# A two-layer encoder trunk on one core: engine order by deadline, buffers from common pools

## The chip, the core and the metric

The kernel runs on one core of a Trainium2 chip. The core has TensorE (PE in the profile, with PEld for its weight loads), VectorE (DVE), ScalarE (ACT), GpSimd (POOL) and SyncE (SP, which here issues almost all DMA). Each engine runs its own instructions in program order and waits on semaphores for the others. The metric is the device time of one execution in microseconds (us). The kernel before takes 858.26 us, the median of three runs (857.68 to 860.0).

## What is computed

Two layers are applied to x, 256 tokens of 2048 channels. All is float32. Cut to what matters:

```python
def hybrid_layer(x, c, cos, sin, layer_idx, w_ada, b_ada, ...):
    mod = (c @ w_ada + b_ada)[:, None, :]
    shift, scale, gate = jnp.split(mod, 3, axis=-1)
    h = rms_norm(x, g_pre) * (1 + scale) + shift
    z = h @ w_in                                    # 2048 x 6144
    u, g_pool, q, k, v, g_diff = jnp.split(z, splits, axis=-1)
    pool_out = multiscale_pool(u, w_pool, pool_scale) * jax.nn.silu(g_pool)
    q, k = apply_rope(q, cos, sin), apply_rope(k, cos, sin)
    att = diff_attention(q, k, v, lam)              # 8 heads, two softmaxes each
    att = rms_norm(att, subln_g) * (1.0 - lam_init)
    diff_out = att.reshape(B, S, D_DIFF) * jax.nn.silu(g_diff)
    y = jnp.concatenate([pool_out, diff_out], axis=-1) @ w_out   # 2048 x 2048
    return x + (1 + gate) * rms_norm(y, g_post)
```

`c @ w_ada` gives 6144 numbers per layer for one vector c; its weights, 50 MB per layer, are as many bytes as w_in's.

## The kernel before

The 256 tokens are two row halves of 128 (`st` 0 and 1), x0 and x1. The large products w_in and w_out are cut into 256 **units**: one unit is a 512 KB piece of weights, 256 rows by 512 columns (`Unit`, with its column block `nb` and its pair of row tiles `k`). w_in has 12 column blocks of 8 units per layer, w_out has 4. Both sides of every product are split in two: `whi`, the weights rounded by an ACT cast, and `wlo`, the rest, raw − whi, by DVE. A unit is then 12 products of 128x512 on PE (24 of 128x256 where the result is wanted transposed): hi by hi, hi by lo and lo by hi. h, the normed and modulated x, is split the same way (`hhi`, `hlo`).

`c @ w_ada` is done on DVE: 192 instructions (`ada`), each multiplying a 512 KB piece by the broadcast c and summing along the row. `ab` makes the columns A and B from them, by which h of a row tile is modulated; so h of row-tile pair `kp` waits for its ada rows, and w_in's units are ordered in visits to the column blocks as h becomes ready. Where a block is visited more than once, its sum is copied out of the accumulator (z<-acc) and back into another (acc<-z), on ACT but for a few of the copies back.

Beside the units run: the rotation of q and k (`rope`), four pairs of attention heads per layer (`heads`), four pooling groups (`pool_group`), the gate's columns turned into a broadcast row `G` (`gate`), and h itself (`make_h`). These are generators. `advance` steps them between units, each when a rough clock (`Clock`) says that its last step is over; `beside` lets them and the ada rows in after each unit, the ada rows by a credit per unit (`RATE`), and `split_to` casts a unit's weights `DEEP` = 2 units ahead. A block's heads begin when its Q, K, V and gate blocks are all done. Buffers are fixed pools by purpose: 12 of z, 9 of h and cat, 4 raw, 3 each of whi and wlo, 3 ada.

The reciprocal square root for the norms before w_in in layer 0 and for the heads is made on POOL (`rsqrt`, with a guess on DVE), that for the residuals on DVE (`rms`).

At the end of a layer, `turn_over` places everything by hand. The last four units of w_out run for half 0 first, then half 1 (`group`). While PE does half 1, half 0 is gated (`end_y`), its residual is added to x0 (`residual`) and squared. Then come half 1's gating, half 0's norm and h (`half_h`), and half 1's residual follows in between. The first four units of layer 1 run for half 0, then for half 1. The ada rows go on during the whole of both layers.

All instructions are issued through one helper, so the profile gives L86 for every row; a row is found by its tile names.

Of the kernel before, what the change touches and what calls it, by code (L numbers as in the profile page):

```python
# [19 lines left out]
DEPTH = 2  # L20
S = 256
# [40 lines left out]
class Unit:  # L62
    def __init__(self, w, l, nb, k, first, last, more):
        self.w, self.l, self.nb, self.k = w, l, nb, k
        self.first, self.last, self.more = first, last, more
        self.extras = []
        self.group, self.far, self.quiet = 0, False, False


class Watched:  # L70


    def __init__(self, clock, key, eng):
        self.clock, self.key, self.eng = clock, key, eng

    def __getattr__(self, name):
        f = getattr(self.eng, name)

        def call(*args, **kw):
# [3 lines left out]
            if "out" not in kw:  # L83
                outs.append(aps.pop(0))
            self.clock.note(self.key, outs, aps + list(named.values()))
# [5 lines left out]
class Clock:  # L91


    FIXED = {"tensor": 0.0, "vector": 0.07, "scalar": 0.09, "gpsimd": 0.15, "sync": 0.0}
    EACH = {"tensor": 0.42e-3, "vector": 1.04e-3, "scalar": 0.85e-3, "gpsimd": 2.3e-3, "sync": 1.43e-3}

    def __init__(self, nc):
        self.now = dict.fromkeys(self.FIXED, 0.0)
        self.wrote, self.used, self.last = {}, {}, 0.0
        for k in self.FIXED:  # L100
            setattr(self, k, Watched(self, k, getattr(nc, k)))

    def note(self, key, outs, ins):
        n = math.prod(outs[0].shape[1:])
        if key == "sync":
            n *= outs[0].shape[0] / P
        if key == "tensor" and ins[-1].dtype == F32:
            n *= 4 if len(ins) == 2 and ins[-1].shape[-1] != P else 2
        t = self.now[key]
        for x in ins:  # L110
            t = max(t, self.wrote.get(x.tensor.name, 0.0))
        for x in outs:
            if key != "tensor":
                t = max(t, self.used.get(x.tensor.name, 0.0))
        t += self.FIXED[key] + n * self.EACH[key]
        self.now[key] = t
        done = t + (1.5 if key == "sync" else 0.15)
        for x in ins:
            self.used[x.tensor.name] = max(self.used.get(x.tensor.name, 0.0), t)
        for x in outs:  # L120
            self.wrote[x.tensor.name] = self.used[x.tensor.name] = done
        self.last = max(self.last, done)


class Kern:
    def __init__(self, ctx, tc, a, out):
        self.tc, self.nc, self.a, self.out = tc, Clock(tc.nc), a, out
        pool = lambda name, bufs, **kw: ctx.enter_context(tc.tile_pool(name=name, bufs=bufs, **kw))
        self.cp = pool("cp", 1)
        self.sp = pool("sp", 2)  # L130
# [7 lines left out]
        self.accp = pool("accp", 4, space=PSUM)  # L138
        self.psp = pool("psp", 4, space=PSUM)
        self.dp = pool("dp", 2, space=bass.MemoryType.DRAM)  # L140
        self.names = 0
        self.live = 0

    def name(self, s):
        self.names += 1
        return f"{s}{self.names}"

    def t(self, pool, shape, tag, dt=F32, **kw):
        return pool.tile(shape, dt, tag=tag, name=self.name(tag), **kw)

    def ps(self):
        self.live += 1
        return self.t(self.psp, [P, 512], "ps")
# [1036 lines left out]
```

## Time and profile before

| | |
|---|---|
| median of three runs | 858.26 us (857.68, 858.26, 860.0) |
| the profiled execution | 856.63 us, span 854.8 us |
| bytes read | 242.17 MB |
| first product of a unit | 25.16 us |
| last w_out product of layer 0 ends, first w_in product of layer 1 | 436.4, 443.74 us |
| last w_out product of layer 1 ends | 844.71 us |

The span runs from the first to the last instruction of the profiled execution; the time of a run is a little longer. The page gives busy time per engine; a window gives the same for a stretch of the span, with the granted clock of PE (PEclk) and what the DMA engines moved. A group row gives all instructions of one kind: how many, their sum in us, the mean of one in ns, and the idle time of the engine right before them with what ended it. In a timeline row the first number is the start, the second the length in us, and the bracket the wait before it.

### The profile page before, as it was taken

The numbers are of one execution on the slowest core, as the hardware profiler recorded it, in microseconds if no ns is written. First come the engines' busy times: TensorE is split into PE (matmuls) and PEld (weight loads), VectorE is DVE, ScalarE is ACT, GpSimd is POOL, SyncE is SP. The second block draws the span as 40 slices with busy tenths as digits, with TensorE's granted clock in tenths as the row PEclk, the third lists the DMA queues.
The fourth block names the chain that finished last, engine by engine and source line by source line (L and its number), as shares of the span: only waits on it lengthen the run. The fifth ranks groups of instructions, "written<-read, shape, count | busy, mean of one in ns | idle before, by whom it ended". The sixth has DMA issues, their size and how long they took to land.

```text
span 854.8 us, 11938 instructions
## 1 busy us (share of the span) xinstructions
PE 803.6 (94%) x4058; PEld 667.5 (78%) x4058; DVE 695.5 (81%) x1194; ACT 543.5 (64%) x950; POOL 45.8 (5%) x129
## 2 busy tenths in 40 slices
PE   3899899999999999998979999999999999889995
PEld 1678688889888887786758888888889898677884
DVE  6789898888898977988786788888789989667665
ACT  4688787766556666664655656776665567666561
POOL 2000000000000001142000000000000000030400
PEclk9999999999999999999989999999999999999998
DMA  9899999999898975688925999999998888443742
GB/s 340 287 396 327 330 370 344 370 367 350 304 355 325 331 251 166 207 287 292 324 73 182 343 365 383 326 346 322 357 326 333 309 320 265 130 148 109 261 148 99
DMA packets 68239, 245.08 MB, mean 287 GB/s; under 512 B 7729, under 2 KB 8017, under 8 KB 67665
## 3 DMA queue, kind: packets, MB, share of 16 engines
q1 hardware_dynamic: 67890, 244.14, 80.3%
q8 instruction: 32, 0.52, 0.3%
q10 hardware_dynamic: 288, 0.17, 0.1%
q14 instruction: 29, 0.24, 0.1%
HBM read 242.17 MB, written 2.11 MB: 286 GB/s over the span
## 4 chain that ended last, share of the span: by engine, by line
PE 75%; DVE 10%; ACT 5%; DMA 4%; POOL 3%; issue 2%; SPq 0%; DVEq 0%; ACTq 0%
PE acc L86 69%; PE ps L86 6%; DVE wlo L86 3%; ACT whi L86 2%; POOL arh L86 2%; DVE ada L86 2%; DMA raw<-in_w_out 1%; ACT t L86 1%; DMA z<-in_w_ada 1%; DVE z L86 1%; DMA ada<-in_w_ada 1%; DVE rt L86 1%; DMA raw<-in_w_in 1%; DVE x L86 1%; ACT sqj L86 1%
## 5 line engine op out<-in xcount | busy, mean ns | idle before, releaser
L86 ACT CAST whi<-raw 128x1024 fp32r<-128x1024 f32 x247 | 259.4, 1053 | 205.1 <-PE acc L86 182.7
L86 DVE TENSOR_TENSOR wlo<-raw,whi 128x1024 fp32r<-128x1024 f32 x247 | 301.3, 1223 | 81.2 <-ACT whi L86 80.7
L86 PE MATMUL acc<-whi,hhi 128*128 128x512 f32 x860 | 344.3, 400 | 6.0 <-ACT hhi L86 2.5
L86 PE MATMUL acc<-whi,hlo 128*128 128x512 f32 x860 | 337.8, 393 | 1.3 <-DVE hlo L86 1.3
L86 PE MATMUL acc<-wlo,hhi 128*128 128x512 f32 x860 | 337.8, 393 | 0.7 <-DVE wlo L86 0.7
L86 DVE SCALAR_TENSOR_TENSOR ada<-ada,cb 128x1024 f32<-128x1024 f32 x184 | 223.7, 1219 | 5.2 <-DMA ada<-in_w_ada 4.8
L86 PEld LDWEIGHTS acc<-whi,hhi 128*128 128x128 f32 x860 | 163.0, 190 | 45.0 <-ACT acc L86 4.4
L86 PEld LDWEIGHTS acc<-whi,hlo 128*128 128x128 f32 x860 | 162.7, 189 | 37.3 <-DVE hlo L86 2.6
L86 PEld LDWEIGHTS acc<-wlo,hhi 128*128 128x128 f32 x860 | 163.1, 190 | 33.8 <-DVE wlo L86 2.1
L86 ACT ACTIVATE z<-acc 128x512 f32<-128x512 f32 x164 | 88.5, 591 | 1.5 <-PE acc L86 1.5
L86 ACT COPY acc<-z 128x512 f32<-128x512 f32 x123 | 68.7, 585 | 3.1 <-DVE rt L86 3.1
L86 PE MATMUL acc<-hhi,whi 128*128 128x256 f32 x256 | 43.1, 288 | 3.1 <-ACT whi L86 2.0
L86 ACT ACTIVATE t<-ps,nm 128x128 f32<-128x128 f32 x64 | 26.0, 420 | 30.9 <-DVE nm L86 30.9
L86 POOL TENSOR_SCALAR arx<-ass 128x4 f32<-128x4 f32 x8 | 4.1, 517 | 728.6 <-ACT sqj L86 728.3
L86 PE MATMUL acc<-hlo,whi 128*128 128x256 f32 x256 | 41.7, 286 | 0.2 <-DVE hlo L86 0.2
L86 PE MATMUL acc<-hhi,wlo 128*128 128x256 f32 x256 | 41.6, 285 | 0.0
L86 PEld LDWEIGHTS acc<-hhi,whi 128*128 128x128 f32 x256 | 36.6, 193 | 5.4 <-ACT whi L86 2.4
L86 PEld LDWEIGHTS acc<-hlo,whi 128*128 128x128 f32 x256 | 35.7, 194 | 0.4 <-DVE hlo L86 0.4
L86 PEld LDWEIGHTS acc<-hhi,wlo 128*128 128x128 f32 x256 | 35.7, 194 | 0.0
L86 PE MATMUL ps<-consts,t 128*128 128x128 f32 x112 | 17.2, 284 | 17.6 <-issue 12.4
L86 PEld LDWEIGHTS ps<-consts,t 128*128 128x128 f32 x112 | 14.0, 147 | 22.0 <-issue 14.1
L86 PE MATMUL ps<-z,z 64*128 64x128 f32 (+1 forms) x128 | 19.1, 371 | 8.3 <-ACT t L86 7.5
(144 smaller groups left out, 596.8 us busy)
## 6 DMA issues: line engine op xcount, KB each, us to landing
raw<-in_w_in SPq DMA_DIRECT2D x192, 512.0 KB, 5.7
ada<-in_w_ada SPq DMA_DIRECT2D x184, 512.0 KB, 5.7
raw<-in_w_out SPq DMA_DIRECT2D x64, 512.0 KB, 4.6
z<-in_w_ada SPq DMA_DIRECT2D x8, 512.0 KB, 11.4
x<-in_x SPq DMA_DIRECT2D x2, 1024.0 KB, 7.6
Gw<-in_w_pool SPq DMA_DIRECT2D x8, 256.0 KB, 6.4
Gw<-gate SPq DMA_DIRECT2D x2, 1024.0 KB, 4.9
out<-x SPq DMA_DIRECT2D x8, 256.0 KB, 2.7
```

What stands on the lines that cost most here:

```text
L86: return f(*args, **kw)
```

## The change

The generators, the credit and `turn_over` go. The program is now some dozens of **parts** that are planned side by side when the kernel is built: each part (`Task`) is a thread that stops at every instruction it wants to issue and says for which engine. `Flow` keeps a plan of when each engine is free and when each operand is ready, from a table of costs. `choose` takes the engine whose next instruction could start first, and `next_of` picks for it, among the parts that wait for that engine, the one with the earliest due time that can start now, unless it would delay one with an earlier due time past it. A due time is made by `need`: the planned time of PE now plus the planned work up to a unit's first step, less an allowance.

The parts are the loads of raw weights, the casts (`cast`), the rests (`rest`), loads of ada (`load_ada`) and the ada rows (`ada`), accumulators and copies back (`prepare`), the products (`products`), each h, each head, each pair of heads, each pooling group, the gate, each row half's residual. They share `Slots`: 34 large tiles for raw, w, ada, z, h, cat and y, with a number kept for raw, w and ada; 12 middle ones; 4 + 4 accumulator banks. Copies, squares and x times its norm go to DVE or ACT, whichever is planned free earlier (`lighter`). The reciprocal square root is on DVE throughout. Heads begin when Q and K are done, and wait inside for V and the gate. The visiting order of the column blocks is the same in both layers ([6, 4, 8, 10, 2, 0, 7, 5, 9, 11, 3, 1]). PE's products and the bytes loaded are the same as before. All rows now come through line 125.

```diff
-        self.zp = pool("zp", 12)
-        self.hp = pool("hp", 9)
-        self.rawp = pool("rawp", 4)
-        self.wp = pool("wp", 3)
-        self.adap = pool("adap", 3)
-        self.tp = pool("tp", 4)
-        self.pp = pool("pp", 2)
+        self.big = Slots(f, pool("zp"), "z", self.BIG, raw=3, w=6, ada=3)
+        self.tmp = Slots(f, pool("tp"), "t", self.TMP)
+        self.wide = Slots(f, pool("gp"), "g", 1)
+        self.banks = Slots(f, pool("psp", space=PSUM), "b", self.BANKS)
+        self.accs = Slots(f, pool("accp", space=PSUM), "c", self.ACCS)
...
-    def beside(self, u):
-        self.advance()
-        self.todo += u.extras
-        while self.todo and (self.nc.now["vector"] <= self.nc.now["tensor"] + self.AHEAD or len(self.todo) > self.TODO):
-            self.ada(*self.todo.pop(0))
...
-    def turn_over(self, l):
...
-        self.end_y(nb, acc, 0)
-        next(g)
-        self.xss = self.t(self.sp, [P, NST, 4], "xss")
-        order = [2, 3, 0, 1]
-        (r,) = self.together(self.rms(yss[:, 0, :], "ya"))
-        self.residual(l, 0, y, r, order)
...
-        half = self.half_h(l, 0)
-        next(half)
-        for i, j in enumerate(order):
-            self.residual(l - 1, 1, y, r, [j])
-            next(half, None)
...
+    def choose(self):
+        best = None
+        for k in self.ENGINES:
+            asks = [t for t in self.tasks if t.ask and t.ask.key == k]
+            if asks:
+                t, at = self.next_of(k, asks)
+                if best is None or at < best[1]:
+                    best = t, at
+        if best is None:
+            raise RuntimeError("all parts wait")
+        self.time = max(self.time, best[1])
+        return best[0]
+    def next_of(self, k, asks):
+        rows = []
+        for t in asks:
+            a = t.ask
+            if a.dep is None:
+                a.dep = self.depends(a)
+            us = a.us + self.TABLE_US * bool(a.table and a.table[0] != self.table)
+            rows.append((t.due(), max(self.now[k], a.dep), us, t))
+        rows.sort(key=lambda r: r[:2])
+        t0 = min(r[1] for r in rows) + self.NEAR[k]
+        for i, (due, at, us, t) in enumerate(rows):
+            if at <= t0 and not any(q[1] < at + us and at + us + q[2] > q[0] for q in rows[:i] if k != "tensor"):
+                return t, at
+        return rows[0][3], rows[0][1]
...
+    def need(self, u, before=0.0):
+        return lambda: max(self.f.now["tensor"], self.f.time) + self.cum[u.step] - self.cum[self.at] - before
...
+    def lighter(self):
+        now = self.f.now
+        return "vector" if now["vector"] < now["scalar"] else "scalar"
+    def copy(self, out, x):
+        if self.lighter() == "vector":
+            self.nc.vector.tensor_copy(out, x)
+        else:
+            self.nc.scalar.copy(out, x)
...
-    def rsqrt(self, ss, n, mul, tag):
-        gp = self.nc.gpsimd
-        x, h = (self.t(self.sp, [P, n], tag + i) for i in "xh")
-        yi = self.t(self.sp, [P, n], tag + "y", I32)
-        y = yi.bitcast(F32)
-        gp.tensor_scalar(x, ss, mul, EPS, op0=ALU.mult, op1=ALU.add)
-        yield y
-        self.guess(yi, x)
+    def rsqrt(self, ss, n, mul, end=None):
+        v = self.nc.vector
+        x, h = self.small([P, n], "rx"), self.small([P, n], "rh")
+        yi = self.small([P, n], "ry", I32)
+        y = yi.bitcast(F32)
+        v.tensor_scalar(x, ss, 0.5 * mul, 0.5 * EPS, op0=ALU.mult, op1=ALU.add)
+        v.tensor_scalar(yi, x.bitcast(I32), -0.5, 0x5F3759DF - (1 << 22) - (1 << 31), op0=ALU.mult, op1=ALU.add)
...
+    def ada_due(self, e):
+        l, nt, i = e
+        if nt >= 32:
+            return self.need(self.first_end[l]["w_out"], 15.0 + 1.3 * (2 * (48 - nt) - i))
+        kt = nt % 16
+        left = 4 * (kt % 2 == 0) + 2 * (nt < 16) + 1 - i
+        return self.need_h(l, kt // 2, 6.0 + 1.3 * left)
+    def load_ada(self):
+        for e in self.adas:
+            l, nt, i = e
+            due = self.ada_due(e)
+            self.f.due(lambda: due() - 4.0)
+            w = self.big.take([P, D // 2], "ada", kind="ada", keep=4)
+            self.nc.sync.dma_start(w, self.a["w_ada"][l, nt][:, i * D // 2 : (i + 1) * D // 2])
+            self.ada_tiles[e] = w
...
+    def cast(self):
+        for u in self.units:
+            self.f.due(self.need(u, 1.5))
+            self.f.wait(lambda: u.raw is not None)
+            hi = self.big.take([P, 2, NB], "whi", F32R, kind="w", keep=4)
+            self.nc.scalar.copy(hi, u.raw)
+            u.hi = hi
+    def rest(self):
+        for u in self.units:
+            self.f.due(self.need(u, -0.2))
+            self.f.wait(lambda: u.hi is not None)
+            lo = self.big.take([P, 2, NB], "wlo", F32R, kind="w", keep=4)
+            self.nc.vector.tensor_tensor(lo, u.raw, u.hi.bitcast(F32), op=ALU.subtract)
+            self.big.give(u.raw)
+            u.lo = lo
...
+    def end_out(self, u, sts):
...
+            f.wait(lambda: self.G[l] is not None)
+        for st in sts:
+            if u.end:
+                nc.scalar.activation(self.sqj, acc[st], AF.Square, accum_out=self.yss[l][:, st, nb : nb + 1])
+                nc.vector.tensor_tensor(y[:, st, :], acc[st], self.G[l][:, nb * NB : (nb + 1) * NB], op=ALU.mult)
+                self.gated[l][st] += 1
+                if self.gated[l][st] == 4:
+                    f.spawn(lambda st=st: self.residual(l, st), self.need(self.steps[min(self.at + 4, len(self.steps) - 1)][0]))
...
+    def residual(self, l, st):
+        nc = self.nc
+        r = self.rms(self.yss[l][:, st, :])
+        order, last = [2, 3, 0, 1], l + 1 == DEPTH
+        for i in range(5):
+            if i < 4:
+                c = slice(order[i] * NB, (order[i] + 1) * NB)
+                x, y = self.x[st][:, c], self.y[l, order[i]][:, st, :]
+                nc.vector.scalar_tensor_tensor(x, y, r, x, op0=ALU.mult, op1=ALU.add)
+                if last:
+                    nc.sync.dma_start(self.out[st * P : (st + 1) * P, c], x)
+            if i and not last:
+                self.square(l + 1, st, order[i - 1])
+        if st:
+            self.big.give(*(self.y[l, nb] for nb in range(4)))
+        if not last:
+            self.xr[l + 1][st] = self.rms(self.xss[l + 1][:, st, :])
```

On DVE at the turnover from layer 0 to layer 1, the order before has half 0's four residual pieces (x010 is x of half 0, z its gated y, yay its norm) ahead of the gating of half 1 (acc872):

```order
L86 SCALAR_TENSOR_TENSOR x010_111<-z841_3958,yay886_4202,x010_111 128x512
L86 SCALAR_TENSOR_TENSOR x010_111<-z858_4048,yay886_4202,x010_111 128x512
L86 SCALAR_TENSOR_TENSOR x010_111<-z876_4135,yay886_4202,x010_111 128x512
L86 SCALAR_TENSOR_TENSOR x010_111<-z880_4170,yay886_4202,x010_111 128x512
L86 TENSOR_TENSOR z880_4170<-acc872_4114,Gw720_3409 128x512
L86 SCALAR_TENSOR_TENSOR t2887_4223,xss881_4197<-x010_111 128x512
```

After, the gating of half 1 (yz469_3604<-accc116) is fourteen rows up, and what follows the last small step of half 1's norm is half 1's residual (x1_10 is x of half 1, x0_9 that of half 0):

```order
L125 SCALAR_TENSOR_TENSOR ry62_4238<-rh61_4237,ry62_4238 128x1
L125 SCALAR_TENSOR_TENSOR x1_10_93<-yz521_3929,ry62_4238,x1_10_93 128x512
L125 SCALAR_TENSOR_TENSOR x1_10_93<-yz538_4026,ry62_4238,x1_10_93 128x512
L125 SCALAR_TENSOR_TENSOR x1_10_93<-yz450_3385,ry62_4238,x1_10_93 128x512
L125 SCALAR_TENSOR_TENSOR x1_10_93<-yz469_3604,ry62_4238,x1_10_93 128x512
L125 SCALAR_TENSOR_TENSOR junkt65_4258,xss2_81<-x1_10_93 128x512
L125 TENSOR_REDUCE rs163_4260<-xss2_81 128x1
```

Eight small steps later half 0's residual comes, with a unit's rest and half 1's h (hz540, hz541) before its last piece:

```order
L125 SCALAR_TENSOR_TENSOR ry66_4272<-rh65_4271,ry66_4272 128x1
L125 SCALAR_TENSOR_TENSOR x0_9_92<-yz521_3929,ry58_4183,x0_9_92 128x512
L125 SCALAR_TENSOR_TENSOR x0_9_92<-yz538_4026,ry58_4183,x0_9_92 128x512
L125 SCALAR_TENSOR_TENSOR x0_9_92<-yz450_3385,ry58_4183,x0_9_92 128x512
L125 TENSOR_TENSOR wloz571_4221<-rawz562_4186,whiz568_4206 128x1024
L125 TENSOR_TENSOR hz540_4036<-hft68_4292,hz540_4036 128x128 x2
L125 TENSOR_TENSOR hz541_4037<-hft69_4296,hz541_4037 128x128 x2
L125 SCALAR_TENSOR_TENSOR x0_9_92<-yz469_3604,ry58_4183,x0_9_92 128x512
L125 SCALAR_TENSOR_TENSOR junkt70_4314,xss2_81<-x0_9_92 128x512
L125 TENSOR_REDUCE rs167_4316<-xss2_81 128x1
```

So half 0, whose residual stood under PE's products of half 1, now stands behind half 1's residual, its square and its norm; its own norm ends 16 rows after these.

On ACT at the start, the order before makes hhi of the first row tile (B, A are the modulation's columns) ahead of the first cast, and the casts of further units behind it:

```order
L86 ACTIVATE hhi_255<-ps_245,B_170,A_168 128x256
L86 ACTIVATE hf_254<-ps_245,B_170,A_168 128x256
L86 CAST whi_260<-raw_187 128x1024
L86 ACTIVATE hhi_255<-ps_245,B_170,A_168 128x256
L86 ACTIVATE hf_254<-ps_245,B_170,A_168 128x256
L86 CAST whi_273<-raw_191 128x1024
L86 CAST whi_279<-raw_195 128x1024
L86 CAST whi_311<-raw_199 128x1024
```

After, the casts of five units stand ahead of it:

```order
L125 CAST whiz_143<-rawz_115 128x1024
L125 CAST whiz_263<-rawz_142 128x1024
L125 CAST whiz_269<-rawz_145 128x1024
L125 CAST whiz_274<-rawz_147 128x1024
L125 CAST whiz_279<-rawz_149 128x1024
L125 ACTIVATE hz_113<-psb_284,B_100,A_98 128x256
L125 ACTIVATE hft_292<-psb_284,B_100,A_98 128x256
L125 ACTIVATE hz_113<-psb_284,B_100,A_98 128x256
L125 ACTIVATE hft_292<-psb_284,B_100,A_98 128x256
```

The first h, which the first product needs, has moved behind the casts of units 0 to 4.

More of the change, by code (lines that the diff above doesn't have):

```diff
@@ L357, in ada @@
[L357 to L373 removed]
+        self.rope_made = True
@@ new lines, in products @@
+    def products(self):
+        f = self.f
+        for n, (u, sts) in enumerate(self.steps):
+            self.at = n
+            f.due(1e9)
+            turned = u.w == "w_in" and u.nb in GP
+            f.wait(lambda: all(u.visit.ready[st] for st in (range(NST) if turned else sts)))
+            self.mm(u, sts)
+            u.left -= len(sts)
+            key = u.w, u.l, u.k // 2
+            if not u.left:
+                self.big.give(u.hi, u.lo)
+                self.uses[key] -= 1
+                if not self.uses[key]:
+                    self.big.give((self.h if u.w == "w_in" else self.cat).pop((u.l, u.k // 2))[0])
+            if turned:
+                sts = list(range(NST)) if sts[-1] else []
+            if u.last and sts:
+                end = self.end_visit if u.w == "w_in" else self.end_out
+                nxt = next((v for v in self.visits if v.at > u.visit.at + 1 and not v.ready[0]), u.visit)
+                f.spawn(lambda u=u, sts=sts: end(u, sts), self.need(self.units[nxt.at], 3.0))
+        self.at = len(self.steps) - 1
```

1479 lines of the change are left out of this document (722 added, 757 removed).

## The prediction

> **What bounds the kernel now.** I read the page's busy times first, then the chain that ended last, then busy time by stage.
>
> ```profile
> span 854.8 us, 11938 instructions
> PE 803.6 (94%) x4058; PEld 667.5 (78%) x4058; DVE 695.5 (81%) x1194; ACT 543.5 (64%) x950; POOL 45.8 (5%) x129
> ...
> PE 75%; DVE 10%; ACT 5%; DMA 4%; POOL 3%; issue 2%; SPq 0%; DVEq 0%; ACTq 0%
> ```
>
> TensorE (PE) is the bound: 94% busy, three quarters of the chain. All that can be won lies in the 854.8 − 803.6 = 51.2 us in which it isn't busy, and all that can be lost lies in new waits of PE. VectorE (DVE) is the next engine, at 81%. The windows below are cut at the stages of the program: start, w_in and w_out of layer 0, the turnover between the layers, w_in of layer 1 in two pieces, its w_out, the tail.
>
> ```profile
> core 0: us, PE busy (x) PEld busy (x) DVE busy (x) ACT busy (x) POOL busy (x), PEclk, DMA share, GB/s
> 0.00:25.20 25.20, 8.32 (x13) 3.22 (x13) 18.03 (x66) 10.86 (x21) 6.28 (x17) 1.00 0.94 351
> 25.20:317.00 291.80, 286.35 (x1465) 241.22 (x1465) 253.76 (x381) 210.01 (x320) 0.00 (x0) 0.99 0.93 339
> 317.00:436.40 119.40, 112.50 (x560) 89.73 (x558) 98.99 (x198) 68.25 (x164) 21.09 (x56) 1.00 0.72 242
> 436.40:443.70 7.30, 1.16 (x5) 0.72 (x4) 6.40 (x31) 4.02 (x11) 0.00 (x0) 0.82 0.00 1
> 443.70:581.80 138.10, 136.95 (x704) 117.11 (x705) 109.93 (x167) 90.13 (x138) 0.00 (x0) 0.98 0.86 311
> 581.80:730.70 148.90, 148.90 (x786) 127.41 (x784) 129.47 (x190) 95.15 (x137) 0.00 (x0) 1.00 0.90 317
> 730.70:844.70 114.00, 109.46 (x537) 88.12 (x533) 72.95 (x148) 64.43 (x162) 18.38 (x56) 0.97 0.45 143
> 844.70:854.80 10.10, 0.01 (x1) 0.00 (x0) 5.96 (x18) 0.69 (x2) 0.00 (x0) 0.63 0.60 197
> ```
>
> PE's time without work: 16.9 us at the start, 6.1 in the turnover, 10.1 in the tail, and some 18 in all the rest (5.5 + 6.9 + 1.2 + 0 + 4.5). Busy time flatters PE where its products come thinly, as two windows of 20 us show:
>
> ```profile
> 80.00:100.00 20.00, 17.61 (x70) 13.07 (x69) 16.46 (x31) 16.27 (x28) 0.00 (x0) 0.91 0.92 310
> 500.00:520.00 20.00, 20.00 (x92) 16.57 (x91) 16.97 (x24) 12.54 (x18) 0.00 (x0) 1.00 1.01 387
> ```
>
> The first is 88% busy but holds 70 rows against 92, so the stalls may be worth twice what the busy time says: some 18 to 36 us outside start, turnover and tail.
>
> **The change part by part.** PE gets the same rows in nearly the same sequence of units, and the bytes loaded are the same. What changes is what stands on DVE, ScalarE (ACT) and the load queue between them. Five terms, in us of the span.
>
> *Start.*
>
> ```profile
> 24.07 1.04 ACT L86 CAST whi<-raw 128x1024 fp32r<-128x1024 f32 x1
> 25.16 1.22 PE L86 MATMUL acc<-hhi,whi 128*128 128x256 f32 x4 [2.04 <-ACT whi L86]
> 30.70 0.40 PE L86 MATMUL acc<-whi,hhi 128*128 128x512 f32 x1
> ```
>
> Before, the first product waits for one cast, and unit 1 starts at 30.70. After, ACT's order puts the casts of units 0 to 4 ahead of the first h. The fifth raw tile stands behind eight ada loads, four raws and the two MB of x: 8.9 MB, which the 351 GB/s of the first window bring by 25.4. With the cast (1.04), the step to h and its product, the first product falls at 27 to 31, and unit 1, now ready at once, 3 later: 30 to 34 against 30.70. I take +2 (0 to +5). The reciprocal root's move from GpSimd (POOL) to DVE gains nothing here: these loads hide it. Without that cover it would gain part of POOL's 6.28.
>
> *Layer 0, w_in* (25.2 to 317.0).
>
> ```profile
> L86 DVE TENSOR_TENSOR wlo<-raw,whi 128x1024 fp32r<-128x1024 f32 x247 | 301.3, 1223 | 81.2 <-ACT whi L86 80.7
> L86 DVE SCALAR_TENSOR_TENSOR ada<-ada,cb 128x1024 f32<-128x1024 f32 x184 | 223.7, 1219 | 5.2 <-DMA ada<-in_w_ada 4.8
> L86 DVE COPY acc<-z 128x512 f32<-128x512 f32 x17 | 11.7, 687 | 0.0
> L86 DVE TENSOR_TENSOR rt<-acc,sin 128x256 f32<-128x256 f32 x32 | 11.9, 415 | 0.0
> ...
> 30.11 3.50 DVE L86 TENSOR_TENSOR wlo<-raw,whi 128x1024 fp32r<-128x1024 f32 x3 [0.51 <-ACT whi L86]
> ```
>
> Copies that were ACT's go to whichever engine the plan thinks freer. In this stage DVE gets 29 more rows of 128x512 (20 us at 687 ns), 23 more of 128x256 (9.5 at 415), 9 more reduces of that size (3.7) and 3 more ada rows (3.7): 37 at busy durations, some 31 where rows follow without a gap (three wlo in 3.50 are 1.17 each, not 1.22; I take 1.17 for a wlo or ada below). DVE goes from 253.8 to about 285 to 291 of 291.8 us: as full as PE. The stalls of this stage (5.5 busy, perhaps 10) can shrink, since heads and h's are placed by due time; but a wlo now often stands behind another piece of DVE work, and there is no slack left to absorb it. I take −5 for the stalls and +4 for the waits: −1 (−8 to +9). If DVE's rows cost their busy durations and it waits 3% of the time, the upper end holds.
>
> *Layer 0, w_out.*
>
> ```profile
> 380.00:400.00 20.00, 17.62 (x80) 13.68 (x78) 16.58 (x35) 9.36 (x15) 9.03 (x22) 1.00 0.84 284
> ```
>
> Here the attention heads' chain goes through POOL (21.09 us busy in the stage) and PE waits 6.9 by busy time, up to twice that by rows. After, block 0's heads run beside w_in (DVE's reduces in this stage go from 29 to 19) and the root is done on DVE in a dozen steps of 0.1 to 0.2. I take −6 (−10 to +2).
>
> *The turnover.*
>
> ```profile
> 434.52 2.74 DVE L86 SCALAR_TENSOR_TENSOR x<-z,yay,x 128x512 f32<-128x512 f32 x4
> 435.37 0.39 PE L86 MATMUL acc<-z,hlo 128*128 128x512 f32 x1
> 436.05 0.39 PE L86 MATMUL acc<-z,hlo 128*128 128x512 f32 x1
> 437.60 0.69 DVE L86 TENSOR_TENSOR z<-acc,Gw 128x512 f32<-128x512 f32 x1 [0.34 <-ACT sqj L86]
> 438.21 0.68 DVE L86 SCALAR_TENSOR_TENSOR t<-x 128x512 f32<-128x512 f32 x1
> 441.30 0.61 DVE L86 TENSOR_SCALAR t<-x,xay 128x256 f32<-128x256 f32 x2
> 443.74 0.79 PE L86 MATMUL acc<-whi,hhi 128*128 128x512 f32 x1 [0.91 <-ACT hhi L86]
> ...
> L86 DVE SCALAR_TENSOR_TENSOR yah<-yay,yau 128x1 f32<-128x1 f32 x6 | 1.3, 220 | 0.2
> L86 DVE SCALAR_TENSOR_TENSOR yay<-yah,yay 128x1 f32<-128x1 f32 x6 | 1.0, 160 | 0.2
> ```
>
> Before, row half 0's residual (434.52) is done while PE still multiplies half 1 (last product ends 436.4). From half 1's gating (437.60) to the next layer's first product (443.74) it is 6.1 us, and PE stands for 7.3. After, the first product of layer 1 still needs half 0 of x, but DVE's order, quoted in the section on the change, has the gating of half 1, then half 1's residual, and only then half 0's. What DVE does from that gating to half 0's scale, at the durations above: gating 0.6; 13 small steps of two interleaved chains 2.2; four residual pieces 2.7; a square 0.6; nine dependent small steps 1.9; three pieces of half 0 2.0; a wlo 1.2; four pieces of h's low part 1.1; the last piece, its square and reduce 1.5; three wlo, two ada and eleven small steps 5 × 1.17 + 11 × 0.15 = 7.5; sum 21.3. Then scale, transposes, modulation and cast, 441.30 to 443.74: 2.4. The gating starts 1.2 after the last product as before. Gap: 24.9; with every small step at its fastest 22.6 (before, 22 of them stand between the square's end at 438.9 and 441.30: 0.11 each); and 35 if DVE comes to the gating late and waits for casts inside. Against 7.3: +17.6, ends +15 and +28. DVE has up to 19 rows more in its order around here (8 wlo, 7 ada) than the walk counts, so I take +22.
>
> *Layer 1 and tail.*
>
> ```profile
> 760.00:780.00 20.00, 18.43 (x91) 14.15 (x92) 12.12 (x30) 10.69 (x31) 3.32 (x12) 0.91 0.27 79
> ```
>
> The stalls in w_out (4.5 busy, up to 9) largely go, as heads are moved into w_in (reduces in w_out 33 before, 3 after): −7. Against it: 59 ada rows stand between units 128 and 176, 34 before. That is 25 × 1.17 = 29 us more for DVE in a stretch that PE needs some 131 us for (48 units × 12 products; three products take 436.05 − 435.37 = 0.68). DVE had 109.9 of 138.1 there; 139 is more than the stretch holds: +5 (0 to +15). The tail keeps its order, 0. Together −2 (−9 to +13).
>
> **Sum**: 2 − 1 − 6 + 22 − 2 = **+15** on the profiled span of 854.8. The profiled execution took 856.63, 1.8 over its span, and lies 1.6 under the median of 858.26; +15 on that median is **873**.
>
> **The rivals.**
>
> 1. *Faster: PE's scattered stalls were worth more than the turnover costs.* Place: w_in of layer 0 and both w_out. If the stalls are 36 rather than 18 and all but a fifth go (−29), the turnover is at its lower end (+15) and start and layer 1 cost nothing, the time is 858 − 14 = 844. It decides from the point where the stalls won exceed 15 to 17. For it: POOL's hop leaves the heads, and heads start sooner. Against: the busy rows show only 18 us, and DVE, nearly full, is what would have to win them. 0.14.
> 2. *DVE becomes the bound over the whole of w_in.* If DVE at 98% makes PE wait 5% in both w_in stages (579 us × 0.05 = 29) rather than what I took (9): 873 + 20 = 893. For it: wlo is needed just in time, and the plan keeps units' wlo at most one ahead where adas crowd. Against: 80.7 us of DVE's waiting before the wlo's was for a cast, so DVE has that much slack to rearrange. 0.18.
> 3. *The loads become the bound.* Between units 128 and 174, 45.6 MB are asked.
>
> ```profile
> ada<-in_w_ada SPq DMA_DIRECT2D x184, 512.0 KB, 5.7
> ...
> 60.00:80.00 20.00, 19.31 (x105) 16.45 (x106) 18.15 (x27) 17.45 (x30) 0.00 (x0) 1.00 0.96 357
> ```
>
> With three ada buffers in flight and 5.7 us to landing plus 1.2 of use, an ada comes each 2.3 us at best; at the 357 to 387 GB/s of full windows, 45.6 MB take 118 to 128 us beside PE's 126. It costs 5 to 10 more: 880. 0.10. The Trainium skill, page "Perfetto Trace Analysis", section "Roofline", says that the 358 GB/s of a core is its share when both cores of a pair load, and that one core alone can pull about 120% of it, up to some 435 GB/s. By that rule 45.6 MB would take an estimated 105 us and this rival would go. The trace lies between: 387 GB/s with the DMA share at 1.01.
> 4. *Gains and losses cancel*: stalls −20, turnover +17, start +2: 857. 0.08. That deadlines don't hold is part of these: the order already shows half 1 ahead of half 0.
>
> **How the numbers follow.** Forecast 873 with a range of its own of 860 to 887 (the root of the squares of the terms' half widths 2.5, 8.5, 6, 6.5 and 11 is 17; these ends are bounds, so I take 14): 0.50. The range 848 to 890 takes that in, the loads' 880, the cancelling 857, nearly half of rivals 1 and 2. A measurement here can tell 0.3%, 2.6 us, from no change: faster 0.14 (rival 1), same 0.08 (rival 4), slower 0.78.
>
> **What would show it.** In the profile of after: a gap of PE between the last w_out product of layer 0 and the first w_in product of layer 1 of 22 to 35 us (7.3 now), with DVE in it on x of half 1 and its square, a wait "PE ps <- DVE/ACT" of that length, and PE's clock under 1 behind it; DVE at 87 to 90% of the span; windows of w_in of layer 0 with DVE at 95% or more; POOL near nothing; unit 1 at 30 to 34. Wrong would be: a gap under 15 us, or DVE under 93% in layer 0's w_in with PE still waiting for wlo.

## The result, and the profile after

The changed kernel takes 865.53 us, the median of six runs (863.28 to 866.97), against 857.74 for the kernel before in the same sitting: a ratio of 1.0089, 95% interval 1.0068 to 1.0111, or 7.8 us slower. The profiled execution took 866.97, the slowest of the six, over a span of 865.2: 10.4 more than the span before. Of these 10.4, some 2.5 are the luck of the two profiled executions (1.4 above its median here, 1.1 below it before). From the page of the changed kernel:

```profile
span 865.2 us, 11872 instructions
PE 802.3 (93%) x4058; PEld 667.1 (77%) x4058; DVE 742.6 (86%) x1375; ACT 509.9 (59%) x871; POOL 0.2 (0%) x4
```

PE has the same work (803.6 before) and stands 62.9 us instead of 51.2. DVE went from 81% to 86%, GpSimd to nothing. The windows are cut at the same places of the program as before: start, w_in and w_out of layer 0, turnover, w_in of layer 1 up to and after unit 176, its w_out, tail.

```profile
core 0: us, PE busy (x) PEld busy (x) DVE busy (x) ACT busy (x) POOL busy (x), PEclk, DMA share, GB/s
0.00:30.00 30.00, 8.56 (x13) 3.20 (x13) 22.70 (x78) 14.47 (x24) 0.20 (x4) 1.00 0.94 363
30.00:317.60 287.60, 285.01 (x1476) 241.26 (x1477) 279.16 (x454) 198.28 (x297) 0.00 (x0) 1.00 0.93 347
317.60:427.30 109.70, 109.67 (x546) 89.27 (x545) 104.48 (x239) 64.13 (x148) 0.00 (x0) 1.00 0.85 303
427.30:453.20 25.90, 2.23 (x8) 1.21 (x8) 24.61 (x69) 14.99 (x34) 0.00 (x0) 0.55 0.68 238
453.20:600.00 146.80, 141.62 (x697) 118.51 (x698) 136.62 (x225) 79.27 (x119) 0.00 (x0) 0.96 0.94 353
600.00:757.50 157.50, 157.50 (x861) 132.20 (x861) 111.92 (x197) 92.09 (x167) 0.00 (x0) 1.00 0.60 191
757.50:855.20 97.70, 97.70 (x461) 81.42 (x460) 57.48 (x104) 45.93 (x84) 0.00 (x0) 1.00 0.36 115
855.20:865.20 10.00, 0.05 (x1) 0.00 (x0) 5.61 (x16) 0.69 (x2) 0.00 (x0) 0.75 0.58 192
```

| stage | before | after | measured | predicted |
|---|---|---|---|---|
| start | 25.2 | 30.0 | +4.8 | +2 (0 to +5) |
| layer 0, w_in | 291.8 | 287.6 | −4.2 | −1 (−8 to +9) |
| layer 0, w_out | 119.4 | 109.7 | −9.7 | −6 (−10 to +2) |
| turnover | 7.3 | 25.9 | +18.6 | +22 (+15 to +28) |
| layer 1 and tail | 411.1 | 412.0 | +0.9 | −2 (−9 to +13) |
| span | 854.8 | 865.2 | +10.4 | +15 |

The stages say where the time went. In both w_out stages and behind unit 176 PE now never waits (109.67 of 109.70, 157.50 of 157.50, 97.70 of 97.70): outside start, turnover and tail it stands 7.8 us (2.6 + 5.2) where it stood 18.0. What this wins is spent, and more, in the turnover, where it stands 23.7 instead of 6.1, and at the start. The turnover in the timeline of the changed kernel, DVE's larger rows and PE's, with three of ACT's that bear on them:

```profile
426.88 0.39 PE L125 MATMUL accc<-whiz,catz 128*128 128x512 f32 x1
427.75 1.21 DVE L125 TENSOR_TENSOR wloz<-rawz,whiz 128x1024 fp32r<-128x1024 f32 x1
427.78 1.04 ACT L125 CAST whiz<-rawz 128x1024 fp32r<-128x1024 f32 x1 [3.27 <-DMA rawz<-in_w_in]
428.73 0.59 ACT L125 ACTIVATE sqj<-accc 128x512 bf16<-128x512 f32 x1
429.01 1.22 DVE L125 SCALAR_TENSOR_TENSOR adaz<-adaz,cb 128x1024 f32<-128x1024 f32 x1
430.23 0.68 DVE L125 TENSOR_TENSOR yz<-accc,Gwg 128x512 f32<-128x512 f32 x1
432.81 2.74 DVE L125 SCALAR_TENSOR_TENSOR x<-yz,ry,x 128x512 f32<-128x512 f32 x4
438.18 2.07 DVE L125 SCALAR_TENSOR_TENSOR x<-yz,ry,x 128x512 f32<-128x512 f32 x3
442.84 0.74 DVE L125 SCALAR_TENSOR_TENSOR x<-yz,ry,x 128x512 f32<-128x512 f32 x1
444.50 1.22 DVE L125 TENSOR_TENSOR wloz<-rawz,whiz 128x1024 fp32r<-128x1024 f32 x1
451.41 1.31 ACT L125 ACTIVATE xnt<-x,ry 128x256 f32<-128x256 f32 x3 [5.56 <-DVE ry L125]
451.97 1.11 PE L125 MATMUL psb<-consts,xnt 128*128 128x128 f32 x4 [12.00 <-ACT xnt L125]
453.21 0.80 PE L125 MATMUL accc<-whiz,hz 128*128 128x512 f32 x1
```

The four pieces at 432.81 are half 1's residual; half 0's come at 438.18 and 442.84. From the gating at 430.23 to the first product at 453.21 it is 23.0 us; the walk along the order gave 21.3 + 2.4 = 23.7. The gating itself starts 3.0 us after the last product, not 1.2, because DVE comes to it late: its rows follow one another without a gap from 424.69 on, and a wlo (427.75) and an ada row (429.01) begin behind PE's last product and ahead of the gating. ACT's square of the same accumulator, behind a cast that waited 3.27 us for a load, is over at 429.4, 0.8 us before the gating begins.

### The profile page after: what moved, and what is told of

It reads as the page before. It is cut to its first block, busy times and chain, and to the rows that moved or that the text cites. A ratio compares the mean times of both kernels' runs of the same rounds, so it can differ in the third digit from the quotient of the medians.

```text
span 865.2 us, 11872 instructions
## 1 busy us (share of the span) xinstructions
PE 802.3 (93%) x4058; PEld 667.1 (77%) x4058; DVE 742.6 (86%) x1375; ACT 509.9 (59%) x871; POOL 0.2 (0%) x4
## 4 chain that ended last, share of the span: by engine, by line
PE 37%; DVE 8%; DMA 4%; issue 2%; ACT 2%; DVEq 0%; SPq 0%; ACTq 0%
PE accc L125 33%; PE psb L125 4%; DVE adaz L125 3%; DVE wloz L125 3%; DMA rawz<-in_w_in 2%; DMA adaz<-in_w_ada 2%; DVE x L125 1%; DVE yz L125 0%; ACT xnt L125 0%; ACT whiz L125 0%; ACT hz L125 0%; DVE rh L125 0%; ACT hft L125 0%; DVE ry L125 0%; ACT zz L125 0%
## 5 line engine op out<-in xcount | busy, mean ns | idle before, releaser
L125 PE MATMUL accc<-whiz,hz 128*128 128x512 f32 x1280 | 408.2, 396 | 2.1 <-ACT hz L125 2.0
L125 ACT CAST whiz<-rawz 128x1024 fp32r<-128x1024 f32 x256 | 264.3, 1051 | 97.8 <-DMA rawz<-in_w_in 49.8
L125 DVE TENSOR_TENSOR wloz<-rawz,whiz 128x1024 fp32r<-128x1024 f32 x256 | 305.9, 1218 | 15.6 <-ACT whiz L125 12.7
L125 PEld LDWEIGHTS accc<-whiz,hz 128*128 128x128 f32 x1280 | 242.0, 190 | 54.4 <-ACT hz L125 2.9
L125 PE MATMUL accc<-wloz,hz 128*128 128x512 f32 x640 | 253.1, 396 | 1.6 <-DVE wloz L125 1.6
L125 DVE SCALAR_TENSOR_TENSOR adaz<-adaz,cb 128x1024 f32<-128x1024 f32 x192 | 229.2, 1218 | 7.2 <-DMA adaz<-in_w_ada 5.3
L125 PE MATMUL accc<-whiz,catz 128*128 128x512 f32 x512 | 161.1, 393 | 0.0
L125 PEld LDWEIGHTS accc<-wloz,hz 128*128 128x128 f32 x640 | 121.6, 190 | 27.7 <-DVE wloz L125 3.5
L125 PEld LDWEIGHTS accc<-whiz,catz 128*128 128x128 f32 x512 | 95.4, 188 | 19.2 <-issue 0.3
L125 PE MATMUL accc<-wloz,catz 128*128 128x512 f32 x256 | 100.5, 393 | 0.0
L125 DVE COPY accc<-zz 128x512 f32<-128x512 f32 x44 | 30.1, 687 | 17.7 <-ACT zz L125 17.5
L125 DVE TENSOR_TENSOR yz<-accc,Gwg 128x512 f32<-128x512 f32 x16 | 10.7, 687 | 27.9 <-ACT sqj L125 27.8
```

The source lines that it names most:

```text
L125: return f(*args, **kw)
```

## The experiments

Theory: the order at the turnover costs the time, and the due times win PE's scattered waits elsewhere. Against it stand three others: DVE's load, the loads from memory, and the new visiting order of the blocks. A ratio is to the kernel before, run beside it. A window is from one execution. How far executions scatter, e1, e10 and e15 show, whose orders are the same up to unit 157: their first products come at 29.4, 28.5 and 30.4, unit 128 at 435.2, 433.6 and 439.4, and units 132 to 153 take 64.8, 67.3 and 67.1. Only w_out of layer 0, where PE never waits, agrees to 0.1.

**e1_x0_first**, half 0's residual due before half 1's:

```diff
-                    f.spawn(lambda st=st: self.residual(l, st), self.need(self.steps[min(self.at + 4, len(self.steps) - 1)][0]))
+                    f.spawn(lambda st=st: self.residual(l, st), self.residual_due(l, st))
...
+    def residual_due(self, l, st):
+        if l + 1 < DEPTH:
+            return self.need(next(u for u in self.units if u.l == l + 1), 10.0 - 5.0 * st)
+        return self.need(self.steps[min(self.at + 4, len(self.steps) - 1)][0])
```

> The changed kernel with one edit: between the layers, the due time of half 0's residual is 10 us before unit 128 and that of half 1's 5 us before it, so that DVE does half 0 first. Theory (the order at the turnover costs the 18.6 us by which PE's gap grew): the gap of 25.9 us before the first product of layer 1 falls to 9 to 12, and the time from 865.5 to 848 to 852. Rival (DVE's larger load, 742.6 us busy against 695.5, sets the time): the gap falls too, but units 128 to 176, which took 146.8 us, grow by as much, since DVE is 93% busy there already; time 858 to 866.

Measured: 856.03 us, ratio 0.9986 (0.9969 to 1.0003); span 854.1, 11.1 under the changed kernel's. The turnover, units 128 to 131, 132 to 153 and 154 to 175, then 176 to 199:

```profile
426.20:435.20 9.00, 1.12 (x4) 0.60 (x4) 8.26 (x26) 5.48 (x14) 0.00 (x0) 0.62 0.95 365
435.20:455.70 20.50, 16.21 (x57) 12.98 (x58) 17.49 (x43) 17.29 (x39) 0.00 (x0) 0.75 0.41 119
455.70:520.40 64.70, 63.61 (x345) 54.55 (x344) 62.92 (x113) 38.07 (x59) 0.00 (x0) 1.00 0.97 359
520.40:588.90 68.50, 63.46 (x302) 52.29 (x300) 60.21 (x87) 37.94 (x53) 0.00 (x0) 0.98 1.00 384
588.90:655.80 66.90, 66.90 (x346) 57.42 (x345) 50.52 (x64) 34.24 (x42) 0.00 (x0) 1.00 0.77 268
```

The gap falls from 25.9 to 9.0, and it is 8.1 to 9.8 in the profiles of e10, e11, e12, e13 and e15, which have the same edit: the order is its cause. Of the 16.9 won, 6.9 are given back by unit 176. Units 128 to 131 take 20.5 instead of 16.6, since half 1's h is late now: PE waits 4.2 us there for its scaled x. Units 132 to 175 take 133.2 instead of 130.2, little more than the scatter. So the theory holds for the cause, and the rival for two fifths of the amount. DVE's load alone doesn't account for it: DVE is busy 97% in units 132 to 153 and 88% in 154 to 175, and the second stretch is the slower one, with the DMA share at 1.00 and 384 GB/s. These are the largest waits of ACT, PE and DVE in e1 between 520 and 589:

```profile
ACT whiz L125 <- DMA rawz<-in_w_in: 22.6, 11, 4.3
PE accc L125 <- DVE wloz L125: 5.0, 4, 2.3
DVE adaz L125 <- PE accc L125: 2.4, 1, 2.4
DVE adaz L125 <- DMA adaz<-in_w_ada: 1.5, 4, 0.7
```

PE's two longest waits (2.3 and 1.6 us) are for a wlo that stands on DVE right behind an ada row, and that ada row had itself waited, 2.4 us in one case and 0.7 for its load in the other. The chain back from there runs over ada loads, not over ACT's casts. In units 132 to 175 of the kernel before (458.6 to 581.8), ACT's casts wait 41.4 us for PE to free their buffers and never for a load.

**e2_h_before_casts**, the start in the changed kernel:

```diff
-            self.f.wait(lambda: u.raw is not None)
+            self.f.wait(lambda: u.raw is not None and (u is self.units[0] or (0, 1, 0) in self.h_hi))
             hi = self.big.take([P, 2, NB], "whi", F32R, kind="w", keep=4)
```

> The changed kernel with one edit: the casts of units 1 and up wait in the plan until the first h is made, so that ACT makes h ahead of them. Theory (the casts ahead of h cost the start): first product from 30.0 to 26 to 27 us, unit 1 from 34.8 to about 31, time 3 to 4 less. Rival (the loads set unit 1 whatever ACT does): first product earlier, unit 1 still at 34 to 35, time within 1 us of 865.5.

Measured: 868.28 us, ratio 1.0146 (1.0103 to 1.0189). First product at 28.4 and unit 1 at 33.2: both 1.6 earlier, and the total no better. But 28.5 to 30.4 is what the start gives without this edit (e1, e10, e15). Within one execution, the first h begins 2.6 us after the last scaled copy of x begins in the changed kernel (26.72 to 29.36), 1.6 in e10 and 1.3 in e2. So casts ahead of h cost 0.3 to 1.3 of the 4.8, and neither theory is right. Rows at the start of the changed kernel show what else stands ahead of h:

```profile
16.40 1.22 DVE L125 SCALAR_TENSOR_TENSOR adaz<-adaz,cb 128x1024 f32<-128x1024 f32 x1
25.00 1.22 DVE L125 SCALAR_TENSOR_TENSOR adaz<-adaz,cb 128x1024 f32<-128x1024 f32 x1
26.72 0.34 DVE L125 TENSOR_SCALAR xnt<-x,ry 128x256 f32<-128x256 f32 x1
29.36 0.56 ACT L125 ACTIVATE hz<-psb,B,A 128x256 fp32r<-128x256 f32 x1
30.41 0.42 DVE L125 TENSOR_TENSOR hz<-hft,hz 128x256 fp32r<-128x256 f32 x1 [1.07 <-ACT hft L125]
```

The first two are the first and the last of eight ada rows. They begin only after the norm's steps, and the scaled copy of x's second half (26.72), which the first h needs, stands behind all eight.

**e11_start**, half 0 first, and those rows moved:

```diff
+            self.f.due(13.0)
             self.nc.vector.tensor_reduce(s1, self.xss[0], axis=AX.X, op=ALU.add)
...
+        if l == kp == 0:
+            f.due(-50.0)
         for st in range(NST):
             self.scaled(xn[:, st, :], self.x[st][:, kp * S : (kp + 1) * S], self.xr[l][st])
+        f.due(self.need_h(l, kp, 4.0))
```

> Half 0 first as in e1, and at the start the norm of x is due later and its scaled copy sooner, so that DVE's order has four ada rows ahead of the norm's small steps, two among them and two behind the scaled copy; in the changed kernel all eight stand between the norm and the second half's scaled copy. Theory (that place of the eight rows costs the start, not the casts): first product from 29.4 to 25 to 26 us, unit 1 from 33.7 to 29 to 30.5, time 3 to 4 under e1's 856.0. Rival (the raw loads, asked behind eight ada loads, set unit 1): first product earlier, unit 1 still at 33 to 34, time within 1 us of e1.

Measured: 857.55 us, ratio 1.0000 (0.998 to 1.0019). First product at 25.0, unit 1 at 30.1: the start is won as expected, clear of the 28.5 to 30.4 without the edit (two casts stand ahead of h now instead of five, so the casts' part is in it). The total is not. w_in of layer 0:

```profile
25.00:318.60 293.60, 287.06 (x1476) 242.03 (x1477) 280.63 (x452) 202.39 (x304) 0.00 (x0) 0.99 0.94 347
```

The stage takes 293.6 (287.2 to 289.6 in e1, e10 and e15) and ends at 318.6, within their 316.0 to 320.0: PE waits 6.5 in it instead of 2.4 to 3.1. What was won at the start is lost inside the stage. Why the rows of the re-made plan make PE wait there, I didn't find.

**e3_old_orders** and **e4_before_new_orders**, the visiting orders exchanged:

```diff
-    ORDERS = [[6, 4, 8, 10, 2, 0, 7, 5, 9, 11, 3, 1]] * 2
+    ORDERS = [[6, 0, 4, 8, 11, 5, 1, 7, 2, 10, 3, 9], [5, 2, 4, 7, 0, 3, 6, 1, 10, 11, 8, 9]]
```

and in the kernel before the reverse.

> The changed kernel with the column blocks visited in the order of the kernel before. Theory (w_out of layer 0 became 9.8 us shorter because the new order of blocks ends the blocks of the first heads early): w_out of layer 0 goes from 109.7 back to 117 to 120 us, time up to 8 more. Rival (it became shorter because parts are placed by due time and the root left GpSimd): w_out stays at 108 to 112, time within 3 us.

> The kernel before with the column blocks visited in the new order, in both layers. Theory (the order of blocks brings the shorter w_out): w_out of layer 0 from 119.4 to about 110 us, time from 857.7 to 848 to 852. Rival (due times and the root on DVE bring it): w_out within 3 us of 119.4 as heads still begin late and go through GpSimd, time 855 to 860.

Measured: e3 881.41 us, ratio 1.0294 (1.0273 to 1.0315); e4 901.72, ratio 1.0549 (1.0508 to 1.0589). Their w_in and w_out of layer 0, e3's ahead:

```profile
28.60:328.60 300.00, 291.21 (x1502) 246.88 (x1502) 288.43 (x470) 205.03 (x306) 0.00 (x0) 1.00 0.93 349
328.60:433.20 104.60, 104.60 (x521) 84.58 (x520) 99.64 (x234) 60.26 (x141) 0.00 (x0) 1.00 0.81 291
...
25.10:335.10 310.00, 295.79 (x1520) 246.98 (x1521) 265.61 (x421) 223.91 (x368) 11.90 (x28) 0.99 0.87 313
335.10:451.00 115.90, 109.18 (x502) 86.47 (x500) 87.92 (x159) 60.49 (x120) 6.97 (x28) 0.97 0.73 266
```

| w_in + w_out of layer 0, us | old order | new order |
|---|---|---|
| hand-placed | 291.8 + 119.4 = 411.2 | 310.0 + 115.9 = 425.9 |
| by due time | 300.0 + 104.6 = 404.6 | 287.6 + 109.7 = 397.3 |

Both theories fall as I put them. With the old order w_out is even shorter (104.6), at the cost of w_in; the new order alone makes the hand-placed kernel 14.7 us worse in these two stages. The due times win 6.6 with the old order, and the new one, which suits them alone, 7.3 more. In e4 another 30 us are lost in layer 1. So the new order is worth having only with the due times. The rest of e3's 16 us lies behind its turnover, where units 128 to 131 take 26.3 us (16.6 in the changed kernel).

**e13_pool_root**, the heads' root back on GpSimd, half 0 first:

```diff
...
-        r = self.rsqrt(ss, 4, 1.0 / P, rr)
+        r = self.rsqrt(ss, 4, 1.0 / P, rr, self.nc.gpsimd)
```

> Half 0 first as in e1, and the reciprocal root of the heads goes back to GpSimd but for its first two steps. Theory (w_out of both layers became shorter because the root left GpSimd): w_out of layer 0 goes from 109.6 to 113 to 118 us, that of layer 1 from 97.7 up too, time 3 to 8 more. Rival (heads begin early enough that their root is hidden anywhere): both within 1.5 us, time within 2 us of e1's 856.0.

Measured: 860.11 us, ratio 1.0034 (1.0014 to 1.0055), some 4 over e1. w_out of layer 0 and of layer 1:

```profile
317.30:428.80 111.50, 109.66 (x546) 89.16 (x544) 103.33 (x208) 63.87 (x147) 20.51 (x52) 1.00 0.86 308
746.00:847.20 101.20, 99.49 (x461) 82.61 (x459) 55.44 (x84) 45.82 (x84) 10.09 (x26) 0.98 0.35 112
```

111.5 against 109.6 and 101.2 against 97.7: the root's move is worth 1.9 and 3.5 us of the two stages' 9.7 and 16.3, less than the theory's 113 to 118 for layer 0, while the time is within its 3 to 8. The larger part is left to the earlier heads and the order of blocks, which no run parts.

**e12_act_copies**, half 0 first, `lighter` always "scalar":

```diff
-        return "vector" if now["vector"] < now["scalar"] else "scalar"
+        return "scalar"
```

> Half 0 first as in e1, and all copies, squares and scaled copies go to ACT, as most did before. Theory (DVE's extra rows cost PE waits in w_in of layer 0, where DVE is 97% busy): the stage shortens from 287 us by 2 to 5 and the time by 3 to 8. Rival (the extra rows on DVE cost nothing there and take load off ACT, whose copies would stand behind casts that wait for loads): the stage lengthens, time 3 to 10 more.

Measured: 856.81 us, ratio 0.9993 (0.9978 to 1.0009), as e1. w_in took 300.7 us, but it began at 22.4, since DVE had no squares ahead of the ada rows, and held 60 rows of PE more, which w_out lost (102.3). The sum of the two is 403.0, against 396.8 in e1. The start won 7.0 and the two stages lost 6.2, so neither theory shows in the total: which engine copies is worth nothing in it. Whether DVE's fill bounded the stage e12 can't tell, since ada rows took the copies' place and DVE is busy 277.6 us in it all the same.

**e10_hold**, half 0 first, ada loads for layer 1's gate held back; **e15_hold150** the same with 150 us:

```diff
             self.f.due(lambda: due() - 4.0)
+            self.f.wait(lambda: l == 0 or nt < 32 or due() < self.f.time + 60.0)
             w = self.big.take([P, D // 2], "ada", kind="ada", keep=4)
```

> Half 0 first as in e1, and the loads of the ada rows for the gate of layer 1 wait until they are due within 60 us. Theory (the loads limit units 132 to 176, since ada rows are fetched there long before they are due: in e1 the DMA share is 0.99 at 372 GB/s and the units take 133.2 us where the kernel before takes 123.2): these units take 123 to 127 us, the DMA share falls under 0.95, and the time goes from 856.0 to 847 to 850. Rival (DVE or the cold clock behind the turnover limits them): they stay at 131 to 134, or what is won there is lost between units 200 and 224, where the held rows go; time 854 to 858.

Measured: 865.9 us, ratio 1.0099 (1.0067 to 1.0131). Units 154 to 175, 176 to 199, 200 to 223:

```profile
520.20:580.60 60.40, 60.40 (x302) 51.47 (x301) 41.19 (x51) 34.95 (x47) 0.00 (x0) 1.00 0.74 236
580.60:647.40 66.80, 66.80 (x345) 57.33 (x344) 39.28 (x46) 29.95 (x36) 0.00 (x0) 1.00 0.67 213
647.40:748.70 101.30, 87.92 (x455) 73.27 (x453) 92.20 (x147) 52.52 (x80) 0.00 (x0) 0.93 0.78 287
```

The held rows free units 154 to 175 (68.5 to 60.4, PE never waits), and cost 10.7 in 200 to 223, where they meet the heads, and some 7 behind. Both theories are half right.

> As e10, but the loads of the ada rows for layer 1's gate wait only until they are due within 150 us: in the order 17 ada rows then stand between units 154 and 176 (27 in e1, 3 in e10) and 18 between 176 and 200 (8 and 3), and no head moves against e1. Theory (the loads alone cost units 154 to 176, which take 68.5 us in e1 at a DMA share of 1.00 and 384 GB/s; what e10 lost behind unit 200 came from rows that met the heads there): units 154 to 176 take 61 to 63 us, 176 to 200 still 67, 200 to 224 still 90.6, time 849 to 852. Rival (any row moved back costs as much later): 154 to 176 shorter, but 176 to 224 longer by as much; time 855 to 858.

Measured: 852.96 us, ratio 0.9935 (0.9912 to 0.9958): faster than both kernels. The profiled execution (856.70) was the slowest of its eight runs. The same three stretches:

```profile
525.90:589.40 63.50, 61.76 (x301) 51.00 (x300) 52.52 (x73) 32.98 (x45) 0.00 (x0) 1.00 0.90 323
589.40:656.60 67.20, 67.20 (x346) 57.30 (x346) 61.69 (x83) 36.72 (x45) 0.00 (x0) 1.00 0.92 355
656.60:747.30 90.70, 90.70 (x518) 74.89 (x517) 70.40 (x151) 60.11 (x129) 0.00 (x0) 1.00 0.53 170
```

Ten ada rows moved by 22 units win 5.0 where the loads were full and cost 0.3 where they had room. The span, 854.9, shows nothing of it beside e1's 854.1, because this execution was already 5.4 us behind e1 at unit 154 (525.9 against 520.4), with the same orders up to there; at unit 224 it is 0.8 behind. That the hold is worth something the medians show: their ratios to the kernel before, 0.9935 here and 0.9986 in e1, have intervals that don't meet. Whether it was the ten loads or the DVE work that moved with them, this run doesn't tell.

**e18_even**, e15 with layer 1's other ada loads held to 60 us as well:

```diff
-            self.f.wait(lambda: l == 0 or nt < 32 or due() < self.f.time + 150.0)
+            self.f.wait(lambda: l == 0 or due() < self.f.time + (150.0 if nt >= 32 else 60.0))
```

> As e15, and the loads of the ada rows for layer 1's h wait until they are due within 60 us. In the order 21 ada rows then stand between units 132 and 154 (29 in e15), 19, 25 and 6 in the next three stretches, and no head moves. Theory (loads asked too early crowd the weights' own loads between units 132 and 176): 132 to 154 goes from 67.1 us to 62 to 64, 154 to 176 stays at 61 to 63, time 846 to 850. Rival (rows of h fetched later make h late, or the plan shifts other rows): PE waits for h there, or the stages before grow; time 853 to 860.

Measured: 854.63 us, ratio 0.998 (0.9961 to 1.0000). Units 132 to 153 take 62.0 as hoped, but 154 to 175 take 72.5: PE waits there for x's scaled copy (2.8) and for wlo (3.8), at a DMA share of 0.89: here it is the order of the rows and not a full queue. The rival.

**e16_rate**, half 0 first, and `MB_US` 0.365 for 0.40; **e17_all**, e11, e15 and e16 together.

> Half 0 first as in e1, and the plan's rate of loads is 0.365 MB per us in place of 0.40; the windows of the changed kernel show 347 to 374 GB/s where the DMA share is 0.93 and more. Theory (a plan that believes loads to be faster than they are puts rows behind casts that still wait: ACT waited 49.8 us for w_in's loads before casts, 8.8 before the change): that wait falls to 20 to 35 us, PE's waits in the load-bound stretches shrink, time 850 to 854. Rival (where the loads limit, the plan's rate changes nothing): the time stays within 2 us of e1's 856.0.

> e11's start, e15's hold and e16's rate together. If all three theories hold and add: first product at 25, units 154 to 176 at 61 to 63, time 843 to 848. If what the start wins is lost again in w_in of layer 0, as in e11, where PE's work fills the stage: 848 to 852. If the loads' share is lost later: 852 to 858.

Measured: e16 859.04 us, ratio 1.0009 (0.9994 to 1.0024); e17 857.89, ratio 0.9997 (0.9979 to 1.0014). In e16 ACT's wait for w_in's loads before casts fell to 25.9 us as expected (59.9 in e1), and the turnover's gap to 6.1. Its units 154 to 175:

```profile
530.50:593.10 62.60, 61.62 (x306) 51.72 (x305) 55.85 (x82) 37.58 (x54) 0.00 (x0) 1.00 1.02 394
```

They take 5.9 less than in e1, and the queue is as full. It brings 24.7 MB here (62.6 us at 394 GB/s) and 26.3 in e1 (68.5 at 384); at 394 GB/s the 1.6 MB between them take an estimated 4 us of the 5.9. DVE's share is the same (89% and 88%). Here DVE never waits for an ada load, and PE waits 1.0 us in all. But w_in of layer 0 takes 302.2 instead of 287.2, as it does in e17 (301.6): PE waits 11.6 us in e16's instead of 2.4, among them 3.7 for a head's rows on ACT and 4.8 for sums that are copied back late. The theory's mechanism holds, its price doesn't, and the parts don't add.

## Why the prediction was right, and where it was off

The sign and the cause were right, and every term lay within its bounds. The sum was twice the difference of the medians: +15 against +10.4 in the spans and +7.8 in the medians. That it came so near is partly luck: each term was off by 2.8 to 3.7 us, two too low and three too high, which leaves 4.6. Of the signs that I named, DVE's 86% of the span (87 to 90 said) and unit 1 at 34.8 (30 to 34) just missed; the gap, the clock behind it, DVE's fill of w_in and the idle GpSimd came.

- *The turnover* decided it, as forecast, and e1 shows that the order is the cause. The walk (gap 24.9) was within 1.0 of the 25.9. The 4.4 us that I laid on it for rows which "DVE has in its order around here" were the error: of those rows one wlo and one ada row came into the gap, ahead of the gating, and made it 1.8 us later; from the gating on, the walk was 0.7 too long. Predicted +22, measured +18.6.
- *w_out of layer 0* was mis-sized: −6 against −9.7. PE waits nothing in it now (6.9 before), and has 2.8 us less work in it. The root's move, which I named, is 1.9 of it (e13); the rest goes with the due times and the block order together (e3, e4).
- *w_in of layer 0*: −1 against −4.2. The +4 for waits behind a full DVE didn't come: DVE is busy 279.2 of 287.6, and PE waits 2.6 (5.5 before). A second engine at 97% didn't make the first wait.
- *The start* had the right range and the wrong reason. I had the casts and the raw loads ahead of h; the casts cost 0.3 to 1.3 of the 4.8 (e2, e10), and e11 wins 3.5 to 5.4 by placing the ada rows otherwise around the norm and x's scaled copy. I had named the root's move as hidden by loads; its steps on DVE (2.1 us, 13.95 to 16.08) are part of what delays the ada rows, which then begin at 16.40 without a wait for their load.
- *Layer 1* was −2 against +0.9. Units 128 to 175 lost 8.7 (I took +5), and I charged DVE for it. DVE's work came as I had counted (136.6 us, 139 said), but the loads, my third rival at 0.10, fit better: the DMA share is 0.99 at 374 GB/s in units 132 to 175 of the changed kernel, the stretch shrinks when its loads are held (e10, e15), and in e1 the slower of two stretches is the one with less of DVE and more of the queue. That isn't shown: holding a row takes its DVE work along, and no run parts the two. Nor is it all: in e1 PE's longest waits are for a wlo right behind an ada row that wasn't ready, and e18 takes 72.5 us, against 60.4 in e10, for units 154 to 175 with room in the queue (0.89). So what the 8.7 are made of stays open. By the Trainium skill a core that loads alone is bounded by its DMA engines at some 435 GB/s ("Perfetto Trace Analysis", section "Roofline"); the windows here stay under that, with e16's 394 at a DMA share of 1.02 the most.
- *The first rival* (faster) was half real: of the 18 us of scattered stalls some 10 went. It needed 15.
- The two profiled executions hid 2.5 of the difference between +7.8 and +10.4. A sum made against one execution can't be better than that, and a single stage's term carries the scatter told above.

## What to carry over

A due time is only as good as the event that it's tied to. Here half 0's residual came due with unit 129 and half 1's with unit 128: each was due with the unit four steps on, and a unit done in two halves counts from its first step. So the half that PE waits for came second; one due time put right gave back 9.5 us of the median. Where a scheduler fetches early, look at what else loads in that stretch: ten ada loads moved on to a stretch with room took 3.1 us off e1's median (e15), and all of the gate's, held to the last 60 us, added 9.9 (e10). And since this scheduler re-makes all that follows an edit, a stage's gain has to be looked for in that stage's window, beside what the same orders give in other executions, and the total has to be measured for each combination.

## What the runs showed that I hadn't expected

Gains of separate stages didn't add up. The start won 4.4 us in e11 and 7.0 in e12, but w_out of layer 0 ended at 428.2 and 425.4, where e1, e10 and e15 end it between 425.6 and 429.6. The same block order was worth −7.3 us to one scheduler and +14.7 to the other. And small edits to the plan changed stages far from them: with the load rate at 0.365, w_in of layer 0 grew by 15 us while the stretch it was meant for shrank by 5.9.
